# One projection of a fp32 backbone as seven products of quarters, with its weight sums made earlier

## The chip, the cores and the metric

The kernel runs on one core of one Trainium2 chip. The metric is the device time of one execution in microseconds, taken as the median of several. The core has five engines with a queue each: TensorE (PE, with its weight loads as PEld), VectorE (DVE), ScalarE (ACT), GpSimd (POOL) and SyncE (SP), which issues nearly all DMAs here. SBUF is the on-chip memory that all engines read, PSUM holds the matmul results in banks of 128 x 512 floats, DRAM is outside.

## The reference

A trunk of two layers over 1024 latent tokens of width 1024, with a prefix of 256 context tokens. The first layer is windowed attention with a gate:

```python
proj = h_lat @ w_in
q = apply_rope(split_heads(proj[..., :q_end], N_Q_HEADS), cos, sin)
...
o = windowed_attention(q, k, v, kc, vc, sink)      # (1, 1024, 16 heads x 128)
y = (o * jax.nn.silu(z)) @ w_out                   # (1024 x 2048) @ (2048 x 1024)
...
x = x + gate * y
```

The second is a convolution module (a projection to 6144 columns, a depthwise convolution of width 31, a layer norm, a projection back), with the same kind of gate, and a last RMSNorm. Everything is float32. The change concerns `(o * silu(z)) @ w_out`, the output projection of the first layer: 1024 tokens by 2048 inputs by 1024 columns.

## The kernel before

**Numbers.** A float32 matrix is held as a high part (rounded to the format fp32r that TensorE takes in one pass) and a low part (the rest, rounded too). A product is three matmuls: high by high, high by low, low by high. The high part is a cast (`act(..., AF.Copy)` on ACT), the low part a subtraction (`split_lo`, on DVE or POOL). One matmul takes a 128 x 128 block and a 128 x 512 block.

**Memory.** Nearly all tiles are pages, `pg.alloc`: 45 pages of 128 x 1024 words in a queue, given out first freed, first used. A new tile therefore waits for the last reader of the page that it takes over. `hp` holds six smaller ones. PSUM is shared out as two tiles of two banks (`ps_s`, pss in the profile), two of one bank (`ps_g`, psg) and two more (`ps_o`, pso).

**Order.** PE runs in program order (`pin("P")`). The instructions of the other engines and of SP are put in order by a planner, which plays the program through on its own estimate of times; where several are ready on an engine, the one earlier in the program goes first. `tc.high_priority()` lifts an instruction, and `after` ties one behind another.

**Attention** runs 128 steps (8 pairs of heads by 16 blocks of 64 tokens). A step makes the scores of the next block on PE, finds the maximum (DVE), takes the exponential (ACT), scales by the reciprocal sum (POOL, the op to which `anchor_p` points), and transposes the block before (PE, then ACT and DVE). Between them `fill` runs a fixed number of matmuls of the input projection. `low_parts` is a generator that is advanced once in most steps: it loads a page of an output weight, makes its low part (ACT cast and POOL subtraction, two of 512 columns each) and stores it in DRAM, in `wolA` for this projection (16 pages) and `wolC` for the last one (16). The gated attention output is stored in DRAM as `ozd`, 16 blocks of 128 rows by 1024 tokens.

**The output projection**, `proj_attn`, works through `seqB`: four quarters of the output (`h`, the half of the tokens, by `m`, the half of the columns), each of 8 steps `kk` of 256 inputs. A step has 4 token blocks `b` with 6 matmuls each, so 24. `load(i)` brings a page of weights, its low part from `wolA` and, if `m` is 0, a page of rows from `ozd`; `split(i)` makes the high weights (ACT) and, if `m` is 0, the high (ACT) and low rows (DVE). `ahead` runs loads two steps and splits one step ahead in program order. Of the first quarter, blocks 0 and 1 of steps 0 to 6 (`EARLY_ROWS`) are run as fill in the last steps of attention. After step 7 of a quarter, `evac0` takes each block out of PSUM: multiply by the gate (DVE), add the residual (DVE or POOL), store to `x1d`, sum the squares (ACT). After the second quarter of a half it also takes the root, scales the rows (`xn`), and puts eight `turn_in` into `later`: transposes of the normalized rows on PE, for the next layer. `bgA` takes these from `later` between steps and loads the first weights of the convolution (`wsB`). The last three steps (`BYBLOCK`) are run block by block.

**The convolution stage** (`b_mm`) follows: 48 column tiles of 2 x 24 matmuls, with the depthwise convolution on DVE, ACT and POOL beside them, and then the last projection.

In the traces all instructions carry the line of one helper (L91), so they are told apart by their tiles: `wo`, `woh`, `wol` are a weight page and its high and low part, `ozf`, `ozh`, `ozl` the same for the rows, `xr` the residual, `x` the new rows, `xn` the normalized ones, `low` and `lhi` the tiles of `low_parts`.

Of the kernel before, what the change touches and what calls it, by code (L numbers as in the profile page):

```python
# [39 lines left out]
LAST_FILL = (11, 10)  # L40
FIRST_FILL = 48
# [55 lines left out]
def backbone_kernel(  # L97
# [619 lines left out]
    wolA, wolC = (dr.tile([2, NK, P, 2, 512], F32, tag=n, name=n) for n in ("wolA", "wolC"))  # L717
# [7 lines left out]
    def store():  # L725
        while made:
            dst, raw = made.pop()
            SY.dma_start(out=dst, in_=raw)
            pg.free(raw)

    def low_parts():

        items = [(pair_rows(w, m, kk), d[m, kk]) for w, d in ((Wo, wolA), (Wp, wolC)) for m in range(2) for kk in range(NK)]
        his = pg.alloc(F32R, [2, 512], "lhi")
        raws = {}

        def load(i):
            if i < len(items):
                raws[i] = pg.alloc(F32, [2, 512], "low")
                SY.dma_start(out=raws[i], in_=items[i][0])  # L740

        for i, (_, dst) in enumerate(items):
            load(i)
            raw = raws.pop(i)
            store()
            yield "open"
            for b in range(2):
                after(act(his[:, b], raw[:, b], AF.Copy), anchor_a)
                after(split_lo(G, raw[:, b], raw[:, b], his[:, b]), anchor_p)
                if b == 0:  # L750
                    yield "open"
            made.append((dst, raw))
            yield "shut"
        store()
        pg.free(his)

    subs = [(h, m) for h in range(2) for m in range(2)]
# [3 lines left out]
    def proj_attn():  # L761

        st, oz = {}, {}
        todo = {"load": 0, "split": 0}

        def load(i):
            s, kk = seqB[i]
            h, m = subs[s]
            w, wl = pg.alloc(F32, [2, 512], "wo"), pg.alloc(F32R, [2, 512], "wol")
            SY.dma_start(out=w, in_=pair_rows(Wo, m, kk))  # L770
            SY.dma_start(out=wl.bitcast(F32), in_=wolA[m, kk])
            st[i] = [w, wl]
            if m == 0:
                f = pg.alloc(F32, [2, 512], "ozf")
                SY.dma_start(out=f, in_=ozd[2 * kk:2 * kk + 2, :, h * 512:h * 512 + 512].rearrange("a p n -> p a n"))
                oz[(h, kk)] = f

        def split(i):
            s, kk = seqB[i]
            h, m = subs[s]  # L780
# [8 lines left out]
            if m == 0:  # L789
                f = oz[(h, kk)]  # L790
                oh, ol = pg.alloc(F32R, [2, 512], "ozh"), pg.alloc(F32R, [2, 512], "ozl")
                high, low = act(oh, f, AF.Copy), split_lo(V, ol, f, oh)
                if 0 < i < EARLY_ROWS:
                    for ins, ties in ((high, (anchor_z[0:1], anchor_a)), (low, (anchor_z[1:2], anchor))):
                        for t in ties:
                            after(ins, t)
                pg.free(f)
                oz[(h, kk)] = (oh, ol)

        def ahead(i, nl, ns):  # L800
            while todo["load"] <= min(i + nl, len(seqB) - 1):
                load(todo["load"])
                todo["load"] += 1
            while todo["split"] <= min(i + ns, len(seqB) - 1):
                split(todo["split"])
                todo["split"] += 1

        def block(s, kk, b, acc, w, o):
            for e in range(2):
                lh, ll = (t[:, e, b * P:b * P + P] for t in o)  # L810
                for a, c in ((lh, w[0]), (lh, w[1]), (ll, w[0])):
                    PE.matmul(acc, a, c[:, e], start=kk == 0 and e == 0 and a is lh and c is w[0],
                              stop=kk == NK - 1 and e == 1 and a is ll)
                    yield

        for i in range(EA):
            ahead(i, 0, -1)
            yield
        ahead(0, 1, 0)
        yield  # L820
        banks = {4: ps_g(), 5: ps_g()}
        for i in range(EARLY_ROWS):
            ahead(i, min(EA, EARLY_ROWS - 1 - i), min(1, EARLY_ROWS - 1 - i))
            for b in range(2):
                yield from block(0, i, b, banks[4 + b], st[i], oz[(0, i)])
# [5 lines left out]
        xr = None  # L831
        for i, (s, kk) in enumerate(seqB):
            h, m = subs[s]
            acc = [banks[b] for b in ((4, 5, 0, 1), (2, 3, 4, 5), (0, 1, 4, 5), (2, 0, 3, 1))[s]]
            ahead(i, EA, 0)
            if kk == 4:
                xr = [pg.alloc(F32, [2, 512], "xr") for _ in range(2)]
                for b in range(4):
                    SY.dma_start(out=xr[b // 2][:, b % 2],
                                 in_=x[0, (4 * h + b) * P:(4 * h + b + 1) * P, m * 512:m * 512 + 512])  # L840
            w, o = st.pop(i), oz[(h, kk)]
            if i >= len(seqB) - BYBLOCK:
                ahead(i, EA, 1)
                held.append((kk, w, o))
                bgA(s, kk)
                if kk == NK - 1:
                    for b in range(4):
                        for k2, w, o in held:
                            run(block(s, k2, b, acc[b], w, o))
                        evac0(s, b, acc[b], xr)  # L850
                    for k2, w, o in held:
                        pg.free(*w, *o)
                continue
            for b in range(2 if i < EARLY_ROWS else 0, 4):
                run(block(s, kk, b, acc[b], w, o))
                if b == 2:
                    ahead(i, EA, 1)
            pg.free(*w)
            if m:
                pg.free(*oz.pop((h, kk)))  # L860
            bgA(s, kk)
            if kk == NK - 1:
                for b in range(4):
                    evac0(s, b, acc[b], xr)
# [3 lines left out]
    def evac0(s, b, acc, xr):  # L868
        h, m = subs[s]
# [4 lines left out]
        if m == 0:  # L874
# [3 lines left out]
        tt(G if b % 2 and s < len(subs) - 1 else V, t, t, xr[b // 2][:, b % 2], ALU.add)  # L878
# [4 lines left out]
        act(junk[:, 0:512], t, AF.Square, accum_out=ss[:, m:m + 1])  # L883
        hp.free(junk)
        if m == 0:
# [3 lines left out]
        for m in range(2):  # L889
            if b % 2 == 0:  # L890
                x1[("n", m, b // 2)] = pg.alloc(F32, [2, 512], "xn")
            V.tensor_scalar(out=x1[("n", m, b // 2)][:, b % 2], in0=x1[(m, b // 2)][:, b % 2], scalar1=r,
                            scalar2=None, op0=ALU.mult)
# [426 lines left out]
    for i, (pr, st) in enumerate(steps):  # L1320
# [36 lines left out]
        if lstate[0] == "open" or h and (h % 4 < 3 or qb < LOWS):  # L1357
# [543 lines left out]
    def bgA(s, kk):  # L1901
        if s == 2 and kk == 6:
            wsB.load()
            wsB.load()
        if s == 3 and kk >= 5:
            wsB.split()
        for _ in range(2 if kk >= 2 or s == 0 and kk else 0):
# [99 lines left out]
```

## Time and profile before

| | |
|---|---|
| median of 3 executions | 1679.54 us (1678.84 to 1679.65) |
| the profiled execution | 1680.83 us, of which 1679.1 us are its span |
| mean granted TensorE clock | 0.999 |
| DMA, all queues | 244.63 MB in 139607 packets, mean 146 GB/s |

The profile shows one execution, cut into 40 slices of 42 us in its overview. Attention fills the slices up to 800 us, the output projection runs from there to 966 us, the convolution stage to 1494 us, the last projection to the end. A busy time of PE is made up of matmuls that overlap: a single 128 x 512 matmul is shown with 390 ns, while they follow each other faster than that. Idle time before an instruction is put down to the instruction or DMA whose semaphore came last.

### The profile page before, as it was taken

The numbers are of one execution on the slowest core, as the hardware profiler recorded it, in microseconds if no ns is written. First come the engines' busy times: TensorE is split into PE (matmuls) and PEld (weight loads), VectorE is DVE, ScalarE is ACT, GpSimd is POOL, SyncE is SP. The second block draws the span as 40 slices with busy tenths as digits, with TensorE's granted clock in tenths as the row PEclk, the third lists the DMA queues.
The fourth block names the chain that finished last, engine by engine and source line by source line (L and its number), as shares of the span: only waits on it lengthen the run. The fifth ranks groups of instructions, "written<-read, shape, count | busy, mean of one in ns | idle before, by whom it ended". The sixth has DMA issues, their size and how long they took to land.

```text
span 1679.1 us, 23843 instructions
## 1 busy us (share of the span) xinstructions
PE 1666.0 (99%) x8340; PEld 1396.3 (83%) x8340; DVE 1091.2 (65%) x2063; ACT 870.2 (52%) x1523; POOL 874.9 (52%) x831
## 2 busy tenths in 40 slices
PE   9999999999999999999999999999999999999998
PEld 6888888888888888888888788888888888888886
DVE  5755554555455554556234389999999999868832
ACT  5644543555355544546333365555665664566731
POOL 0246673576547564642001268999898887130400
PEclk9999999999999999999999999999999999999999
DMA  9424442444335443457976522020211212387981
GB/s 382 171 62 144 141 144 76 142 154 151 105 125 167 148 129 98 127 159 262 325 247 215 193 88 101 1 76 14 76 50 51 88 38 70 132 276 246 318 288 50
DMA packets 139607, 244.63 MB, mean 146 GB/s; under 512 B 44650, under 2 KB 61346, under 8 KB 139488
## 3 DMA queue, kind: packets, MB, share of 16 engines
q1 hardware_dynamic: 133408, 233.15, 40.7%
q10 hardware_dynamic: 6080, 9.97, 2.4%
q8 instruction: 65, 1.06, 0.2%
q14 instruction: 54, 0.44, 0.1%
HBM read 190.90 MB, written 41.69 MB: 139 GB/s over the span
## 4 chain that ended last, share of the span: by engine, by line
PE 97%; DVE 1%; DMA 1%; POOL 0%; ACT 0%; issue 0%; ACTq 0%; POOLq 0%; DVEq 0%
PE psg L91 50%; PE pss L91 26%; PE pso L91 22%; DMA rope_half<-rope_half 1%; POOL rope_half L91 0%; DVE rq L91 0%; DVE x_page L91 0%; DVE ms L91 0%; DVE rope_half L91 0%; POOL kl_page L91 0%; DVE wlo_page L91 0%; ACT whi_page L91 0%; ACTq L91 0%; ACT rope_half L91 0%; DVE hf_page L91 0%
## 5 line engine op out<-in xcount | busy, mean ns | idle before, releaser
L91 POOL TENSOR_TENSOR odd_half<-odd_half,prod_half 128x513 f32<-128x513 f32 (+2 forms) x252 | 314.5, 1256 | 22.5 <-ACT prod_half L91 9.2
L91 POOL TENSOR_TENSOR wlo_page<-wraw_page,whi_page 128x512 fp32r<-128x512 f32 (+1 forms) x104 | 174.9, 1698 | 157.2 <-ACT whi_page L91 125.7
L91 PE MATMUL psg<-hh_page,whi_page 128*128 128x512 f32 x600 | 236.8, 395 | 0.0
L91 PE MATMUL psg<-hl_page,whi_page 128*128 128x512 f32 x600 | 234.8, 391 | 0.0
L91 PE MATMUL psg<-hh_page,wlo_page 128*128 128x512 f32 x600 | 234.3, 390 | 0.0
L91 ACT ACTIVATE prod_half<-ubuf,dww 128x513 f32<-128x513 f32 (+2 forms) x252 | 165.6, 675 | 116.7 <-POOL odd_half L91 113.0
L91 PE MATMUL psg<-h2h_page,whi_page 128*128 128x512 f32 x464 | 181.9, 392 | 0.0
L91 PE MATMUL psg<-h2h_page,wlo_page 128*128 128x512 f32 x464 | 180.6, 389 | 0.0
L91 PE MATMUL psg<-h2l_page,whi_page 128*128 128x512 f32 x464 | 180.6, 389 | 0.0
L91 DVE SCALAR_TENSOR_TENSOR pss<-ubuf,dww,pss 128x512 f32<-128x512 f32 (+3 forms) x270 | 173.0, 674 | 0.1
L91 DVE SCALAR_TENSOR_TENSOR pss<-ubuf,wsum,pss 128x512 f32<-128x512 f32 (+3 forms) x270 | 172.3, 674 | 0.2
L91 ACT ACTIVATE pt<-pss 128x640 fp32r<-128x640 f32 (+1 forms) x128 | 86.7, 677 | 142.5 <-PE pss L91 142.5
L91 POOL TENSOR_SCALAR p_page<-p_page,sc 128x576 f32<-128x576 f32 (+2 forms) x128 | 93.2, 728 | 106.9 <-DVE sc L91 104.4
L91 ACT ACTIVATE p_page<-p_page,sc 128x577 f32<-128x577 f32 (+2 forms) x128 | 96.9, 757 | 78.6 <-DVE sc L91 76.7
L91 DVE CUSTOM_DVE_ANT_0 p_page<-pss,mask_page,nsink 128x576 f32<-128x576 f32 (+1 forms) x112 | 90.2, 806 | 70.5 <-PE pss L91 57.4
L91 PEld LDWEIGHTS psg<-hh_page,wlo_page 128*128 128x128 f32 x600 | 112.7, 188 | 24.2
L91 PEld LDWEIGHTS psg<-hh_page,whi_page 128*128 128x128 f32 x600 | 112.7, 188 | 19.7 <-ACT hh_page L91 0.3
L91 PEld LDWEIGHTS psg<-hl_page,whi_page 128*128 128x128 f32 x600 | 113.0, 188 | 19.1 <-DVE hl_page L91 0.2
L91 DVE TENSOR_TENSOR pt<-pss,pt 128x640 fp32r<-128x640 f32 (+1 forms) x128 | 100.7, 787 | 36.3 <-ACT pt L91 36.1
L91 ACT ACTIVATE whi_page<-wraw_page 128x1024 fp32r<-128x1024 f32 x88 | 92.6, 1052 | 53.9 <-PE psg L91 19.3
L91 PE MATMUL pso<-h2h_page,whi_page 128*128 128x512 f32 x304 | 118.3, 389 | 0.0
L91 PE MATMUL pso<-h2l_page,whi_page 128*128 128x512 f32 x304 | 118.3, 389 | 0.0
(255 smaller groups left out, 3915.6 us busy)
## 6 DMA issues: line engine op xcount, KB each, us to landing
wraw_page<-in_k_wconv_dram SPq DMA_DIRECT2D x48, 512.0 KB
wraw_page<-in_k_win_dram SPq DMA_DIRECT2D x40, 512.0 KB
wo_page<-in_attn_w_out_dram SPq DMA_DIRECT2D x32, 512.0 KB
wol_page<-wolA SPq DMA_DIRECT2D x32, 512.0 KB
wo_page<-in_conv_w_out_dram SPq DMA_DIRECT2D x32, 512.0 KB
wol_page<-wolC SPq DMA_DIRECT2D x32, 512.0 KB
rope_half<-rope_half ACTq DMA_DIRECT2D x76, 128.0 KB
araw_page<-in_k_ada_dram SPq DMA_DIRECT2D x16, 512.0 KB
```

What stands on the lines that cost most here:

```text
L91: r = f(*a, **k)
```

## The change

The 2 x 2 x 2 partition of the projection has row quarters A11, A12, A21, A22 (half of the tokens by half of the inputs) and weight quarters B11 to B22. Before, each of the four output quarters was the sum of two products of quarters, eight in all. Now seven products are made, in Winograd's form:

- round 0, 8 steps: M1 = A11 B11 (steps 0 to 3), kept; then M2 = A12 B21 (steps 4 to 7). C11 = M1 + M2
- round 1, 4 steps: (A21 + A22 - A11) (B22 - B12 + B11). With M1 it makes U2
- round 2: (A21 + A22) (B12 - B11). With U2 it makes U4
- round 3: (A12 - (A21 + A22 - A11)) B22. C12 = U4 + this
- round 4: (A11 - A21) (B22 - B12). C22 = U4 + this, and U3 = U2 + this
- round 5: A22 (B21 - (B22 - B12 + B11)). C21 = U3 + this

The four weight sums are made in `low_parts`, on POOL, from two pages at a time, and stored in DRAM (`wsums`); the low parts of the second column half of this weight are no longer made there. The row sums are made on DVE in `split`. Rounds 1 to 5 load no low parts: weights and rows are both split in the stage, the weights' low parts on POOL. The kept products are copied or added out of PSUM into pages (`m1`, `u2`, `u4`) and added to the residual, times the gate, on POOL (`joined`). In `evac0` the second half of `xn` moves from DVE to ACT, and POOL adds the residual in the first quarter only. `low_parts` starts three steps earlier in attention.

```diff
+LOAD_TO = {0: (8, 7), 1: (8, 7), 2: (9, 7), 4: (9, 8), 5: (10, 8), 6: (10, 8), 7: (11, 9)}
...
+        u = pair(0)
+        yield "open"
+        for kt in range(KT):
+            store()
+            t = pair(kt + KT)
+            minus(u[:, 1], u[:, 0], u[:, 0])
+            yield "open"
+            minus(t[:, 1], u[:, 1], u[:, 1])
+            yield "open"
+            minus(t[:, 1], u[:, 0], t[:, 1])
+            keep(u, (0, 2), kt)
+            yield "open"
+            store()
+            if kt + 1 < KT:
+                u = pair(kt + 1)
+            minus(t[:, 0], t[:, 1], t[:, 0])
+            keep(t, (3, 1), kt)
+            yield "shut"
...
+    SEQA = [(0, kk) for kk in range(NK)] + [(r, kk) for r in range(1, 6) for kk in range(NK // 2)]
...
+            rows = {1: ((1, kk), (1, k2), (0, kk)), 2: (), 3: ((0, k2),), 4: ((0, kk), (1, kk)), 5: ((1, k2),)}[r]
+            st[i] = [o_raw(*a) for a in rows] + [w_raw(pair_rows(Wo, 1, k2) if r == 3 else
+                                                       wsums[{1: 1, 2: 0, 4: 2, 5: 3}[r], kk])]
...
+            if r == 1:
+                a21, a22, f = rows
+                tt(V, a21, a21, a22, ALU.add)
+                pg.free(a22)
+                tt(V, f, a21, f, ALU.subtract)
+                kept[(1, kk)], kept[(2, kk)] = a21, f
+                keep = True
...
+            act(wh, w, AF.Copy)
+            act(oh, f, AF.Copy)
+            wl, ol = pg.alloc(F32R, [2, 512], "wol"), pg.alloc(F32R, [2, 512], "ozl")
+            for e in range(2):
+                split_lo(G, wl[:, e], w[:, e], wh[:, e])
+            split_lo(V, ol, f, oh)
...
+            start, stop = kk % 4 == 0, kk % 4 == 3
...
+        def joined(us, xrs, m, keep=False):
+            ns = slice(m * 512, m * 512 + 512)
+            for b in range(4):
+                u = us[b // 2][:, b % 2]
+                g = hp.alloc(F32, None, "ug")
+                tt(G, g[:, 0:512], u, gbc0[0][:, ns], ALU.mult)
+                for xr in xrs:
+                    t = xr[b // 2][:, b % 2]
+                    tt(G, t, t, g[:, 0:512], ALU.add)
...
+        order = [(0, 2), (0, 3), (1, 2), (1, 3), (2, 2), (3, 2), (2, 3), (3, 3)]
+        order += [(i, b) for i in range(4, EARLY_ROWS) for b in (2, 3)] + [(7, b) for b in range(4)]
+        acc = [banks[b] for b in (4, 5, 0, 1)]
+        for i, b in order:
+            if b == 2 and i != 3:
+                ahead(*LOAD_TO[i])
...
+            run(block(i, b, acc[b]))
+            if i == 3:
+                act(half_pages(m1, b, "m1"), acc[b], AF.Copy)
+            if b == 3:
+                done(i)
+                bgA(0, i)
+                if i == 4:
+                    joined(m1, [xr], 0, True)
...
+        for i in range(8, len(SEQA)):
+            r, kk = SEQA[i]
+            acc = [banks[b] for b in ((2, 3, 4, 5) if r < 4 else (0, 1, 2, 3))]
+            ahead(i + 3, i)
...
+            if (r, kk) == (3, 1):
+                joined(u4, [xr12, xr22], 1)
...
+            for b in range(4):
+                run(block(i, b, acc[b]))
+                if kk == 3 and r in (1, 2, 4):
+                    with tc.high_priority():
+                        d = {1: u2, 2: u4, 4: u2}[r]
+                        d = half_pages(d, b, "u") if r < 4 else d[b // 2][:, b % 2]
+                        tt(V, d, acc[b], (m1 if r == 1 else u2)[b // 2][:, b % 2], ALU.add)
+                if b == 2:
+                    ahead(i + 3, i + 1)
...
+            if kk == 3 and r > 2:
                 for b in range(4):
+                    evac0(r - 3, 1, b, acc[b], xr12 if r == 3 else xr22)
...
+            if (r, kk) == (4, 3):
+                joined(u2, [xr], 0)
...
-        tt(G if b % 2 and s < len(subs) - 1 else V, t, t, xr[b // 2][:, b % 2], ALU.add)
+        tt(G if b % 2 and h == 0 and first else V, t, t, xr[b // 2][:, b % 2], ALU.add)
...
+            if m:
+                act(d, f, AF.Copy, scale=r)
+            else:
+                V.tensor_scalar(out=d, in0=f, scalar1=r, scalar2=None, op0=ALU.mult)
...
-        if lstate[0] == "open" or h and (h % 4 < 3 or qb < LOWS):
+        if lstate[0] == "open" or i >= 5 and (h % 4 < 3 or qb < LOWS):
```

More of the change, by code (lines that the diff above doesn't have):

```diff
@@ L788, in split @@
             st[i] = (wh, wl)
[L789 to L796, printed above, removed]
+            f = oz[i]
@@ new lines, in residual @@
+        def residual(h, m):
+            xr = [pg.alloc(F32, [2, 512], "xr") for _ in range(2)]
+            for b in range(4):
+                SY.dma_start(out=xr[b // 2][:, b % 2],
+                             in_=x[0, (4 * h + b) * P:(4 * h + b + 1) * P, m * 512:m * 512 + 512])
+            return xr
+        def joined(us, xrs, m, keep=False):
[7 more added lines that the diff above has]
+                    tt(G, t, t, g[:, 0:512], ALU.add)
+                hp.free(g)
+                if b % 2 and not keep:
+                    pg.free(us[b // 2])
@@ L1899, in backbone_kernel, with bgA @@
     projB = proj_out()
-    def bgA(s, kk):
-        if s == 2 and kk == 6:
+    def bgA(r, kk):
+        if (r, kk) == (4, 3):
             wsB.load()
             wsB.load()
-        if s == 3 and kk >= 5:
+        if r == 5 and kk:
             wsB.split()
-        for _ in range(2 if kk >= 2 or s == 0 and kk else 0):
+        for _ in range(2 if r == 0 and kk or r == 4 and kk >= 2 or r == 5 and kk < 2 else 0):
             if later:
```

203 lines of the change are left out of this document (123 added, 80 removed).

## The prediction

> **What bounds the kernel now.** The page comes first: busy shares, slices, and the chain that ended last.
>
> ```profile
> span 1679.1 us, 23843 instructions
> ...
> PE 1666.0 (99%) x8340; PEld 1396.3 (83%) x8340; DVE 1091.2 (65%) x2063; ACT 870.2 (52%) x1523; POOL 874.9 (52%) x831
> ...
> DVE  5755554555455554556234389999999999868832
> ...
> POOL 0246673576547564642001268999898887130400
> PEclk9999999999999999999999999999999999999999
> ...
> PE 97%; DVE 1%; DMA 1%; POOL 0%; ACT 0%; issue 0%; ACTq 0%; POOLq 0%; DVEq 0%
> ```
>
> TensorE is 97% of the chain, at full granted clock throughout. So a matmul taken away is time gained, as long as nothing else becomes late. Slices 19 to 23 are the output projection: DVE and POOL, full in the convolution behind it, stand at 0 to 4 tenths there. Next, the projection's stretches (us, then busy time and instructions of PE, PEld, DVE, ACT, POOL, then clock, DMA share, GB/s).
>
> ```profile
> 804.00:828.50 24.50, 24.50 (x119) 19.88 (x118) 5.50 (x12) 8.15 (x9) 0.65 (x9) 1.00 0.89 321
> 828.50:872.00 43.50, 43.50 (x194) 36.02 (x193) 8.08 (x12) 13.52 (x17) 2.73 (x2) 1.00 0.77 263
> 872.00:920.80 48.80, 48.80 (x233) 40.78 (x232) 25.71 (x54) 21.72 (x34) 8.99 (x7) 1.00 0.64 220
> 920.80:948.00 27.20, 27.20 (x121) 22.52 (x121) 4.36 (x8) 9.29 (x14) 1.71 (x2) 1.00 0.72 264
> 948.00:966.00 18.00, 16.98 (x75) 13.73 (x75) 12.32 (x18) 5.88 (x10) 9.47 (x4) 1.00 0.24 88
> ```
>
> PE waits once, for 1.02 us, in the last stretch. POOL works 23.6 us of 162: room for new work.
>
> **What is removed.** The groups by form (count, busy us, mean ns, idle before) and one piece of the chain of waits (start, us):
>
> ```profile
> L91 PE MATMUL psg<-wol_page,ozh_page 128*128 128x512 f32 x96 | 37.5, 391 | 0.0
> L91 PE MATMUL psg<-woh_page,ozl_page 128*128 128x512 f32 x96 | 37.5, 391 | 0.0
> L91 PE MATMUL psg<-woh_page,ozh_page 128*128 128x512 f32 x96 | 37.4, 390 | 0.0
> L91 PE MATMUL pss<-woh_page,ozh_page 128*128 128x512 f32 x160 | 62.9, 393 | 1.0 <-DVE x_page L91 1.0
> L91 PE MATMUL pss<-wol_page,ozh_page 128*128 128x512 f32 x160 | 62.3, 389 | 0.0
> L91 PE MATMUL pss<-woh_page,ozl_page 128*128 128x512 f32 x160 | 62.3, 389 | 0.0
> ```
>
> ```profile
> 920.79 35.38 PE pss L91 x156
> ```
>
> These are 3 x (96 + 160) = 768 matmuls, 32 steps of 24. The mean of 390 ns is latency, since they overlap; the pace is 35.38 / 156 = 0.2268 us, or 5.44 us a step. The new order has 8 + 5 x 4 = 28 steps, 672 matmuls. Removed: 96 x 0.2268 = **21.77 us**, all on the path. The 84 matmuls inside attention stay as they were; so do the 108 of round 0 behind it (24.5 us). Rounds 1 to 5 then take 20 x 5.44 = 108.8 us, plus 32 transposes of the next input.
>
> **What is added, in the stage.** Every step of rounds 1 to 5 now splits weights and rows into high and low halves itself, where before the low weight half was loaded and rows were split in every second product alone.
>
> ```profile
> L91 POOL TENSOR_TENSOR low_page<-low_page,lhi_page 128x512 f32<-128x512 f32 x64 | 83.1, 1299 | 61.0 <-ACT lhi_page L91 54.0 <-ACT p_page L91 5.4 <-DMA wsum_raw<-in_ada_w_dram 1.6
> L91 ACT ACTIVATE woh_page<-wo_page 128x1024 fp32r<-128x1024 f32 x63 | 66.3, 1055 | 85.0 <-DMA wo_page<-in_conv_w_out_dram 35.9 <-DMA wo_page<-in_attn_w_out_dram 27.2 <-PE psg L91 11.9
> ```
>
> ```profile
> 826.86 0.69 DVE L91 TENSOR_TENSOR x_page<-x_page,xr_page 128x512 f32<-128x512 f32 x1
> ...
> 857.47 1.23 DVE L91 TENSOR_TENSOR ozl_page<-ozf_page,ozh_page 128x1024 fp32r<-128x1024 f32 x1 [12.94 <-PE psg L91]
> ```
>
> - ACT: two casts a step, 2 x 1.06 = 2.1 of 5.44 us; hidden. Half of the xn scalings move here from DVE, also hidden.
> - POOL: two low halves a step, 2 x 1.30 = 2.6 us. The joins add two operations a block for M1 (8, 10.4 us, in round 0), three for U4 (12, 15.6 us, in round 3) and two for U3 (8, 10.4 us, in round 5). Rounds 1 to 5 sum to 20 x 2.6 + 15.6 + 10.4 = 78.0 us, with four h2l (5.2) and two residual adds (2.6) 85.8 of some 112 us. Alone it fits.
> - DVE: one low half a step (1.23) and row sums of the same size: two a step in round 1, one in rounds 3 and 4. That is 32 x 1.23 = 39.4 us, plus 12 sums out of PSUM at 0.69 and evacuations as before. Alone it fits.
>
> The two together are the question, because they do not run side by side:
>
> ```profile
> 952.69 7.68 POOL L91 TENSOR_TENSOR wlo_page<-wraw_page,whi_page 128x1024 fp32r<-128x1024 f32 x3 [28.89 <-DMA wraw_page<-in_k_wconv_dram]
> ```
>
> ```profile
> 952.83 2.82 DVE L91 TENSOR_TENSOR x_page<-x_page,xr_page 128x512 f32<-128x512 f32 x1
> ...
> 956.44 1.49 DVE L91 SCALAR_TENSOR_TENSOR ms<-ssf 128x1 f32<-128x1 f32 x1 [0.79 <-ACT junk_half L91]
> ```
>
> ```profile
> 828.27 1.29 POOL L91 TENSOR_TENSOR x_page<-x_page,xr_page 128x512 f32<-128x512 f32 x1 [23.75 <-DVE x_page L91]
> 831.64 1.67 POOL L91 TENSOR_TENSOR x_page<-x_page,xr_page 128x512 f32<-128x512 f32 x1 [2.08 <-issue]
> ```
>
> A 0.69 us add on DVE takes 2.82 us, ending 0.4 us after the first of the POOL operations (2.56 each) should have ended; a one-column operation takes 1.49, to the end of the second. The other way, 1.29 on POOL becomes 1.67. So DVE operations that read two SBUF tiles and POOL operations wait for each other, whole instructions long. The Trainium skill says the same on its page "SBUF — State Buffer", section "Who interferes with whom": a DVE operation with two SBUF inputs and a GpSimd read exclude each other for the whole instruction. By that rule the sum goes by the joint total below, as these rows do.
>
> The joint total up to where PE can be held up: in the last round the final three steps run block by block, so their splits are due 5.44 + 2.72 = 8.2 us into round 5, that is 87.0 + 3.5 (transposes) + 8.2 = 99 us behind round 0. By then, from full durations: POOL splits and DVE work of 20 steps, 52.0 + 39.4 = 91.4, less two steps of round 1 made in round 0 (2 x 6.3 = 12.6), plus U4's join 15.6, residual adds 2 x 1.3 + 10 x 0.69 = 9.5, h2l 4 x 1.3 + 4 x 0.69 = 8.0: 112 us, 13 too many. But the 2.82 row ended 0.4 us behind its blocker, against 0.69 alone, so about 0.25 us of each operation is start and drain that overlaps. With 18 x 2 + 12 + 2 + 4 = 54 POOL operations on the port, 0.25 less each gives 98 us: full, without overflow. Bounds 0 to 13; I take **4 us** of PE stall, nearer to the lower end, because the 2.82 row speaks for the overlap, and above 0 because a resource that is full to the brim hits some deadlines late.
>
> **Loads.** Round 1 loads four pages a step, 4 x 0.524 MB in 5.44 us, 385 GB/s. The transfers' rate from 804 to 840, in slices of 0.9 us:
>
> ```profile
> GB/s 77 127 259 342 320 331 123 32 173 309 200 262 357 407 389 391 421 410 407 403 410 437 414 423 419 405 401 421 419 398 382 223 259 178 332 412 353 207 255 305
> ```
>
> Pressed, the queue moves about 410 GB/s for 15 us on end. Row 7, round 1 and a residual are 1.6 + 8.4 + 1.0 = 11.0 MB, 27 us, due over some 35. No stall (bounds 0; 7 us at the 263 GB/s of the second stretch). The Trainium skill's page "DMA: Bandwidth & Descriptors", section "Specifications", gives about 358 GB/s as a core's limit to HBM; the row above shows more. By 358 the round's 8.4 MB would take an estimated 23.4 us against 21.8, 1.6 us late without the early loads.
>
> **What is added in attention.** POOL low operations become 32 differences and 24 x 2 low halves, 80 in place of 64: 16 x 1.30 = 20.8 us over 640 us of a POOL that is half busy; ACT loses 16 casts. SP carries 8.4 MB more, and its stores queue behind POOL as before. What PE lost there so far:
>
> ```profile
> PE pss L91 <- POOL p_page L91: 1.6, 1, 1.6
> ```
>
> One wait in 128 steps: the softmax has slack. A POOL operation queued behind the scaling delays the next scaling by 1.3 us at most. I take 0.5 us (bounds 0 and 20.8). M1's copy out of PSUM is a new wait for PE, since step 4 restarts the bank: ACT sits in the softmax queue, and behind ACT's copy wait its exp and transposed copies. Inside attention six matmuls (1.4 us) lie between, against a copy of about 0.6 us:
>
> ```profile
> L91 ACT ACTIVATE pt<-pss 128x512 fp32r<-128x512 f32 x32 | 19.0, 595 | 24.9 <-PE pss L91 24.9
> ```
>
> I take 0.5 us for all four (bounds 0 and 4 x 1.06, one cast ahead of each). Behind the stage U3's join feeds the last evacuations; PE meets them again in the transposes two steps (10.9 us) into the convolution, so that much lateness costs nothing. Banks between rounds have three blocks (4.1 us) against 0.69 on DVE: nothing. The convolution starts earlier with everything it feeds on, so it only shifts; a gain or loss of 2 us by reordering is the bound.
>
> **Sum.** 21.77 - 4 - 0.5 - 0.5 = 16.77 us. The profiled execution took 1680.83 (span 1679.1), 1.3 above the median of 1679.54. 1680.83 - 16.77 = 1664.1; on the median's scale 1679.54 - 16.77 = **1662.8**.
>
> **Rivals.**
> - *Clean*: the splits run so far ahead that nothing is late. Against it: kept sums leave fewer free pages. For it: before, rows of the second half (due at 872, the third stretch above) were cast 30 us ahead:
>
> ```profile
> 842.22 1.06 ACT L91 ACTIVATE ozh_page<-ozf_page 128x1024 fp32r<-128x1024 f32 x1 [0.29 <-DMA ozf_page<-ozd]
> ```
>
>   1679.54 - 21.77 = 1657.8.
> - *POOL's queue order*: U4's 12 joins (15.6 us) run ahead of the split of round 3's third step, due 10.9 us into the round and then done at 15.6 + 2.6 = 18.2: 7.3 us. U3's 8 joins ahead of the last three splits: 10.4 + 7.8 - 8.2 = 10.0. Together 17.3: 1675. For it: both joins stand ahead of these splits in the program; against it: the planner starts what is ready first.
> - *The other side, the shared port without overlap*: from round 1 on, every DVE sum waits out a POOL operation. Full durations for the rounds are 112 + 10.4 (U3) + 2.5 (two convolution splits) = 125 against 112, and each of the 32 DVE operations that meets a POOL one in flight waits on average 0.65 us: 21 more, in DVE's queue ahead of evacuations. 13 + 21 = 34 at worst, 1692; it decides once more than 21.8 us of it, two thirds, reach PE. With three quarters, 26 us, it gives 1684. Against it: DVE is idle enough to wait.
> - *Attention pays*: the added 20.8 us of POOL lie on the path: 1678, no gain. Against it: the single wait above.
>
> **Chances.** Forecast (1660 to 1668) 0.50; clean 0.22; POOL's order 0.14; port 0.08; attention 0.03; in between 0.03. A measurement of this kernel can tell about 0.2%, 3.4 us. Faster by more: 0.87, within: 0.05, slower: 0.08. The range runs from clean less 1.3 to POOL's order nearly whole: 1656.5 to 1674, leaving out the port, attention and the end of POOL's order.
>
> **What would show it.** 672 matmuls on woh and wol tiles of this product; PE's idle time in rounds 1 to 5 by releaser: wol (POOL) or ozl (DVE) for the port; wol alone in rounds 3 and 5 for the queue's order; ozf or wo DMA for loads; xn for late evacuations. POOL and DVE means there above 1.30 and 1.23 show the exclusion. If PE idles under 1 us in the stage, clean was right; if attention's end shifts past 804, POOL there was mispriced.

## The result, and the profile after

The changed kernel takes 1705.05 us (median of 4, 1702.51 to 1705.29), the kernel before 1679.60 beside it (4 runs, 1678.84 to 1679.72): a ratio of 1.0149, interval 1.0131 to 1.0167. It is 25.5 us slower, where 1662.8 was predicted with a range of 1656.5 to 1674. The profiled execution took 1705.04 us, span 1703.3.

The page of the changed kernel: totals, slices of PE, DVE and POOL, granted clock by slice.

```profile
span 1703.3 us, 23865 instructions
...
PE 1657.2 (97%) x8244; PEld 1385.0 (81%) x8244; DVE 1155.3 (68%) x2099; ACT 876.3 (51%) x1527; POOL 1002.7 (59%) x911
...
PE   9999999999999999999799699999999999999998
...
DVE  5755554555355544565657979999999999867832
...
POOL 0247673666547573742659857999898888130300
PEclk9999999999999999999799899999999999999999
```

The 96 matmuls are gone (8340 to 8244). What is new stands in slices 19 and 22 of PE: 7 and 6 tenths, with the clock down to 7 and 8 tenths there. Where it was lost is read off one instruction, the first matmul of the convolution stage (start, duration), before and then after:

```profile
965.46 0.39 PE L91 MATMUL psg<-h2h_page,whi_page 128*128 128x512 f32 x1
```

```profile
989.67 0.39 PE L92 MATMUL psg<-h2h_page,whi_page 128*128 128x512 f32 x1
```

It comes 24.21 us later, and the span is 24.2 longer: all of the loss lies ahead of it. As 21.8 us of matmuls were taken out there, 46 us of something else came in. A little of it is attention's: the first matmul behind attention starts at 805.55 us, before at 803.87, so 1.7 later. The rest belongs to the projection's stage, from that matmul to the first of the convolution: 184.1 us, before 161.6. PE's waits over the whole span (us in all, times, longest):

```profile
PE pss L92 <- ACT m_page L92: 11.0, 2, 9.8
PE pso L92 <- DVE ssf L92: 6.8, 1, 6.8
PE pss L92 <- DVE u_page L92: 6.1, 4, 2.3
PE pss L92 <- DVE x_page L92: 5.5, 3, 2.4
PE pso L92 <- DVE xn_page L92: 3.3, 2, 2.7
...
PE pss L92 <- POOL p_page L92: 2.0, 2, 1.8
```

Before, the stage had one wait of 1.0. The first five rows sum to 32.7 us. Most of the rest of the 46 goes with the clock: in the stage PE is busy for 20.8 us at half clock, where a matmul takes 0.43 us in place of 0.2268, an estimated 10 us lost. The longest wait shows how it comes about. First the timeline of PE at it, then the stretches around it (us, busy of PE, PEld, DVE, ACT, POOL, clock, DMA share, GB/s):

```profile
824.51 0.79 PE L92 MATMUL pss<-woh_page,ozh_page 128*128 128x512 f32 x1 [9.81 <-ACT m_page L92]
825.10 0.63 PE L92 MATMUL pss<-wo_page,ozh_page 128*128 128x512 f32 x1
825.53 0.63 PE L92 MATMUL pss<-woh_page,ozl_page 128*128 128x512 f32 x1
```

```profile
814.00:824.00 10.00, 0.70 (x4) 0.24 (x2) 7.00 (x7) 3.09 (x4) 2.57 (x2) 0.65 0.73 241
824.00:836.00 12.00, 10.29 (x28) 7.39 (x29) 5.50 (x8) 2.95 (x4) 9.01 (x7) 0.50 0.89 284
836.00:840.00 4.00, 4.00 (x16) 3.17 (x15) 2.91 (x2) 0.96 (x1) 4.00 (x2) 0.82 1.05 393
840.00:864.00 24.00, 24.00 (x108) 19.88 (x107) 19.58 (x18) 12.89 (x19) 20.48 (x11) 1.00 0.74 245
```

PE stood 9.81 us, and went on at 0.43 us a matmul (825.53 less 825.10) in place of 0.2268. Why it stood is told by ACT's timeline, and ACT's by DVE's:

```profile
814.07 1.06 ACT L92 ACTIVATE ozh_page<-ozf_page 128x1024 fp32r<-128x1024 f32 x1 [9.00 <-DMA ozf_page<-ozd]
815.03 1.04 ACT L92 ACTIVATE woh_page<-wo_page 128x1024 fp32r<-128x1024 f32 x1
822.92 1.06 ACT L92 ACTIVATE ozh_page<-ozf_page 128x1024 fp32r<-128x1024 f32 x1 [6.84 <-DVE ozf_page L92]
823.88 0.58 ACT L92 ACTIVATE m_page<-pss 128x512 f32<-128x512 f32 x1
```

```profile
817.89 1.91 DVE L92 TENSOR_TENSOR ozf_page<-ozf_page,ozf_page 128x1024 f32<-128x1024 f32 x1 [1.51 <-DMA ozf_page<-ozd]
820.13 1.23 DVE L92 TENSOR_TENSOR ozf_page<-ozf_page,ozf_page 128x1024 f32<-128x1024 f32 x1 [0.33 <-DMA ozf_page<-ozd]
821.28 0.47 DVE L92 COPY dww<-pso 128x124 f32<-128x124 f32 x2
821.67 2.35 DVE L92 TENSOR_TENSOR ozf_page<-ozf_page,ozf_page 128x1024 f32<-128x1024 f32 x2
```

M1's copy takes 0.58 us, but stands in ACT's queue behind the cast of a row of round 1, which waits for DVE's row sums, which wait for the DMA of the rows. The waiting matmul isn't the restart of the copied bank, as one might think. That bank belongs to block 2; the matmul is still one of M1, step 2 of block 3, in the other bank of the same two-bank tile, and the program gives it a wait on ACT's copy.

### The profile page after: what moved, and what is told of

Read it like the earlier page. It is cut to its first block, busy times and chain, and to the rows that moved or that the text cites. A ratio compares the mean times of both kernels' runs of the same rounds, so it can differ in the third digit from the quotient of the medians.

```text
span 1703.3 us, 23865 instructions
## 1 busy us (share of the span) xinstructions
PE 1657.2 (97%) x8244; PEld 1385.0 (81%) x8244; DVE 1155.3 (68%) x2099; ACT 876.3 (51%) x1527; POOL 1002.7 (59%) x911
## 5 line engine op out<-in xcount | busy, mean ns | idle before, releaser
L92 PE MATMUL pso<-h2h_page,wlo_page 128*128 128x512 f32 x304 | 118.4, 390 | 0.0
```

The source lines that it names most:

```text
L92: r = f(*a, **k)
```

## The experiments

Each ran once, beside the kernel before on the same chip (1678.84 to 1679.53); "after" is the changed kernel, 1705.05. Four runs of it span 2.8 us, so smaller differences are not read.

**The wait on M1's copy.** Theory: PE waits for the bank that is restarted.

*e1_own_banks*, M2's blocks 2 and 3 in banks of their own:

```diff
                 act(half_pages(m1, b, "m1"), acc[b], AF.Copy)
+                acc[b] = banks[b]
...
-            acc = [banks[b] for b in ((2, 3, 4, 5) if r < 4 else (0, 1, 2, 3))]
+            acc = [banks[b] for b in ((0, 1, 4, 5) if r < 4 else (2, 3, 0, 1))]
```

> The changed kernel, with M2 of blocks 2 and 3 accumulated in two free PSUM banks, so that TensorE does not wait there for M1's copy. Theory (the copy stands in ScalarE's queue behind a cast that waits for a row sum): the 11.0 us of waits on m_page go, and with them the half clock behind them (about 14 us of half speed, 8 us), so 1705 - 19 = 1686. Rival (the loads are late whatever waits for them): TensorE waits in round 1 for its first row sums instead, 1698 to 1705.

1708.06 us, and the wait on m_page stays at 10.0. The theory falls. It led to the reading above: the matmul that waits is in the tile being read.

*e5_m1_tile* copies a tile only after both of its banks are done, with e1's banks:

```diff
-            if i == 3:
-                act(half_pages(m1, b, "m1"), acc[b], AF.Copy)
+            if (i, b) == (3, 3):
+                for c in (2, 3):
+                    act(half_pages(m1, c, "m1"), acc[c], AF.Copy)
+                    acc[c] = banks[c]
```

> The changed kernel, with both copies of M1's blocks 2 and 3 issued behind step 3 of both blocks, and M2 of these blocks in the other two-bank PSUM tile. Theory (a matmul into one bank of a two-bank tile waits for a reader of the other bank, so step 2 of block 3 waited for the copy of block 2): the 11.0 us of waits on m_page go, with the half clock behind them: 1684 to 1690. Rival (late loads): the idle time comes back in round 1 as waits on ACT woh or ozh, POOL wol or DVE ozl, 1698 to 1706.

1706.37 us. PE's waits in it:

```profile
PE pss L92 <- DVE u_page L92: 11.7, 4, 7.7
...
PE pso L92 <- DVE dww L92: 4.1, 1, 4.1
```

m_page is gone from the list, which shows the tile as the reason for that wait. But its 11 us came back: 4.1 on the copy of the convolution's taps (dww), which stands behind the same row sums on DVE, and 5.6 more on the additions for U. The rival was right: a victim was removed, not the lateness.

**The clock.** *e2_spin* and *e7_spin_ahead* put 44 matmuls whose results are not used into the wait, in e2 ahead of block 2 of step 4, in e7 ahead of the matmul that waits. The edit of e7:

```diff
+            if (i, b) == (2, 3):
+                for _ in range(44):
+                    PE.matmul(banks[2], st[6][0][:, 0, 0:P], oz[6][0][:, 0], start=True, stop=True)
             run(block(i, b, acc[b]))
```

> The changed kernel, with 44 added matmuls (10.0 us at full clock) into an unused bank just ahead of the matmul that waits for M1's copy; their result is not used. Theory (the half clock comes from TensorE standing idle): the wait stays but is filled, the granted clock stays at 1.00 from 814 to 840 us, and about 8 us are gained, 1697. Rival (the clock falls for another reason, or the slow stretch costs nothing because loads set the pace there): 1705, or up to 1715 where the added matmuls lie on the path.

> The changed kernel, with 44 added matmuls (10.0 us at full clock) into an unused bank ahead of step 2 of block 3, which is the matmul that waits for M1's copy; their result is not used. Theory (the half clock comes from TensorE standing idle): the wait is filled, the granted clock stays at 1.00 through 840 us, and 6 to 9 us are gained on the changed kernel's 1705: 1696 to 1699. Rival (loads set the pace in that stretch): 1703 to 1706.

e2 took 1711.12 us: its matmuls stood behind the wait, which stayed at 9.2, so it tells nothing of the clock. e7 took 1709.42. Its stretches:

```profile
814.00:824.00 10.00, 10.00 (x45) 8.29 (x45) 7.83 (x8) 2.96 (x4) 2.79 (x3) 1.00 0.82 270
824.00:836.00 12.00, 10.60 (x51) 8.24 (x50) 8.72 (x8) 2.49 (x3) 12.00 (x8) 1.00 0.98 359
...
840.00:864.00 24.00, 21.02 (x92) 16.76 (x90) 18.07 (x17) 13.55 (x19) 20.65 (x12) 1.00 0.64 213
```

The clock stays at 1.00 through the wait, and nothing is gained: PE, at full pace from 824 on, waits again by 864, where the changed kernel, after its half pace, is busy throughout (24.00 of 24.00 us from 840 to 864). The stage takes 183.9 us, as good as the changed kernel's 184.1; the 4.4 us by which e7 is slower lie in the convolution and behind it (718.7 us from its first matmul to the end, 713.6 in the changed kernel). So the slow clock in round 0 is a consequence of waiting, and cost nothing of its own here, where the data for round 1 were later still.

**Tiles and joins.** *e6_tiles*: e5, and each addition for U issued after both banks of its tile are done (`for c in {1: (0, 1), 2: (2,), 3: (3,)}.get(b, ())`), and round 5's banks in the order 4, 2, 5, 3, so that its evacuations alternate between tiles. *e8_tiles_evac*: also the joins moved from POOL into the evacuation on DVE, where the kept product is added straight to PSUM:

```diff
-    def evac0(h, m, b, acc, xr):
+    def evac0(h, m, b, acc, xr, us):
...
-        tt(V, t, acc, gbc0[0][:, ns], ALU.mult)
+        tt(V, t, acc, us[b // 2][:, b % 2], ALU.add)
+        tt(V, t, t, gbc0[0][:, ns], ALU.mult)
...
-                    joined(m1, [xr], 0, True)
...
-                joined(u4, [xr12, xr22], 1)
...
-                joined(u2, [xr], 0)
```

*e12_taps_later*: e8 with the taps' transposes in round 2, one a step.

> As e5_m1_tile, and besides the sums out of PSUM in rounds 1, 2 and 4 are issued behind the second block of a two-bank tile, and round 5 alternates between tiles. Theory (shared tiles cause the waits on u_page, 6.1 us, and x_page, 5.5 us, too): these go as well, 1668 to 1676. Rival (they come from DVE being late whichever tile is next): the waits stay within 3 us of 11.6, 1682 to 1690.

> As e6_tiles, and M1, U4 and U3 are added in the evacuation on DVE, straight from PSUM, in place of the joins on POOL (28 POOL operations less, 16 DVE operations more). Theory (POOL and DVE hold each other up in rounds 3 to 5, which delays the scaled rows that the transposes wait for): the waits on ssf and xn, 10.1 us, shrink below 4: 1660 to 1668. Rival (DVE is the bound by its own count of operations): as e6_tiles or slower.

> As e8_tiles_evac, with the taps' transposes (whose bank is freed by a copy on DVE that stands behind a row sum) moved from round 0 to round 2. Theory (in-order queues pass the wait for round 1's rows on to whatever short instruction stands behind): the wait on dww, 4.6 us, goes and 2 to 5 us are gained, 1689 to 1692. Rival (it comes back as another wait): 1693 to 1695.

1696.02, 1694.18 and 1695.57. The tiles are worth 9.0 us, about a quarter of what was expected; with the joins it is 10.9, too little more to be read. The 10.9 is what is left of a larger gain: e8's stage is 14.9 us shorter (169.2), and from the convolution on it takes 4.7 longer (718.3). In e12 the wait on dww goes, and u_page rises from 9.0 to 12.1 us, with one of 9.2: passed on again.

**The preparation of rounds 1 to 5.** Four runs that start from the changed kernel. *e3_no_joins* leaves out the joins of U4 and U3 (both `joined` calls become `pg.free`); *e4_no_row_sums* the four `tt(V, ...)` of the row sums; *e11_dve_splits* leaves out nothing, but makes the weights' low halves on DVE:

```diff
-            for e in range(2):
-                split_lo(G, wl[:, e], w[:, e], wh[:, e])
             split_lo(V, ol, f, oh)
+            split_lo(V, wl, w, wh)
```

*e16_after_loads_only* leaves out the row sums and, with `G.memset(wl.bitcast(F32), 0.0)` in place of POOL's two subtractions, the weights' low halves.

> The changed kernel without the joins of U4 and U3 into the residuals (20 POOL operations of rounds 3 to 5): three of the four output quarters lack these terms. Theory (POOL and DVE hold each other up in rounds 3 to 5): most of TensorE's 22 us of waits behind 850 us go, and the half clock around 965 us with them: 1688 to 1692. Rival (DVE's own work is too much): 1702 to 1705.

> The changed kernel without the 16 row sums on DVE: rows are split as they are loaded, so that products 3 to 6 are of other matrices. Theory (DVE's sums stand in the way twice: ahead of the cast before M1's copy, and against POOL later): about half of both waits goes, 1685 to 1692. Rival (late loads and POOL alone set the waits): 1700 to 1705.

> The changed kernel with only one thing altered: the weights' low halves in rounds 1 to 5 are made on DVE, one subtraction of 128x1024 in place of two of 128x512 on POOL. Theory (shared port): faster than 1705 although DVE gets 20 operations more, 1688 to 1697. Rival (DVE is the bound by its own count): 1705 to 1715.

> The changed kernel itself (its tiles and joins as they are) with the four row sums and the weights' low halves left out, as in e13. Port as the main cause: 1705.05 - 13.3 - 13.5 = 1678, 1674 to 1682, the rest of the 46 us being the tiles and late loads. If tiles and loads are the main cause: 1688 to 1692, no better than the run without row sums (1691.75).

1695.39 (9.7 off), 1691.75 (13.3), 1698.49 (6.6) and 1689.03 (16.0). e4 came within what its theory gave; e3 and e11 fell just short of theirs. e11 is the most telling: it puts 20 more instructions on DVE, which is 68% busy in the changed kernel's stage (126.0 of 184.1 us), and is faster. But row sums and splits together give 16.0, hardly more than the sums alone, as the side of tiles and loads had it. Its waits tell why:

```profile
PE pss L92 <- ACT m_page L92: 6.9, 2, 4.2
PE pss L92 <- DVE u_page L92: 4.4, 4, 1.6
```

The tile waits remain, so the same two cuts were made in e8's order: *e9_no_pool_split* (the memset alone), *e13_loads_only* (memset, and no row sums). *e10_all_dve* does the whole computation, with none of the stage's work on POOL: e8 with e11's split, the other POOL instructions of the stage on DVE, and e12's taps.

> As e8_tiles_evac (1694), with the 40 subtractions on POOL that make the weights' low halves in rounds 1 to 5 replaced by 20 memsets to zero, which read nothing from SBUF; the low halves of these weights are left out of the products. Theory (the shared reads of POOL and DVE set the pace of rounds 1 to 5): DVE operations go back to 1.23 us from 2.3 and the waits on u_page, hf and xn mostly go, 1668 to 1676. Rival (late pages and loads set the pace): 1690 to 1695.

> As e8_tiles_evac, with everything that POOL did in the stage moved to DVE (weights' low halves as one 128x1024 subtraction, residual adds, h2l), and the taps' transposes moved from round 0 to round 2. Theory (a pair of pages costs the shared port 1.23 us on DVE and 2.6 on POOL, so DVE alone is faster than both): 1662 to 1674. Rival (DVE's count of operations is the bound: round 1 has some 31 us for it against 21.8 of TensorE): 1685 to 1700.

> The tiles and the joins of the run e8 (1694.18), with the four row sums left out and the weights' low halves left out (a memset in place of POOL's two subtractions), so that of the preparation in rounds 1 to 5 only the loads, ACT's casts and DVE's low half of the rows remain. If the sums and the splits set the pace of the stage, both go: e4 gave 13.3 and e9 gave 13.5, so 1694.2 - 26.8 = 1667, 1662 to 1672. If loads that land late set it, nothing is gained over e9 (1680.66): 1677 to 1682, with PE waits that end in ACT's casts or DVE's splits behind ozf or wo loads.

1680.66, 1691.63 and 1675.02; e9 and e13 lie between what the theory and the rival gave. POOL's subtractions cost 13.5 us here (1694.18 - 1680.66), the row sums 5.6 more. What stands behind the 13.5 is in the groups by form from 804 to 965 (count, busy us, mean ns of one), in the changed kernel and then in e9:

```profile
L92 DVE TENSOR_TENSOR ozl_page<-ozf_page,ozh_page 128x1024 fp32r<-128x1024 f32 x21 | 33.8, 1610 | 26.5 <-ACT ozh_page L92 18.7 <-POOL wol_page L92 3.7 <-issue 1.6
L92 DVE TENSOR_TENSOR ozf_page<-ozf_page,ozf_page 128x1024 f32<-128x1024 f32 x16 | 26.4, 1658 | 18.9 <-DMA ozf_page<-ozd 15.9 <-PE psg L92 2.9
...
L92 POOL TENSOR_TENSOR wol_page<-wo_page,woh_page 128x512 fp32r<-128x512 f32 x40 | 68.0, 1724 | 35.5 <-ACT woh_page L92 17.8 <-issue 8.1 <-DMA xr_page<-in_x_dram 4.1
```

```profile
L92 DVE TENSOR_TENSOR ozl_page<-ozf_page,ozh_page 128x1024 fp32r<-128x1024 f32 x21 | 25.6, 1221 | 15.6 <-ACT ozh_page L92 8.7 <-PE psg L92 5.7 <-POOL h2l_page L92 1.1
L92 DVE TENSOR_TENSOR ozf_page<-ozf_page,ozf_page 128x1024 f32<-128x1024 f32 x16 | 20.6, 1292 | 24.2 <-DMA ozf_page<-ozd 12.8 <-PE psg L92 9.6 <-issue 1.7
```

Beside POOL's reads DVE's splits and sums take 1610 and 1658 ns, without them 1221 and 1292 (in e8, which differs from e9 in the splits alone, 1544 and 1523); POOL's take 1724, where the same shape took 1299 in the kernel before. That is 21 x 0.39 + 16 x 0.37 + 40 x 0.42 = 31 us more of busy time in the changed kernel. It isn't work: an instruction that waits for the other engine's is shown as busy, as the last section shows on single ones. But the queue behind it stands meanwhile. Giving DVE everything doesn't help enough: e10's instructions take 1.22 us, and its stage is 6.3 us shorter than e8's (162.9), but 3.5 of that are lost again from the convolution on (721.8), and its stretches are short of DVE:

```profile
830.00:850.00 20.00, 17.78 (x78) 14.07 (x77) 18.93 (x25) 12.61 (x18) 0.00 (x0) 1.00 0.71 253
...
930.00:950.00 20.00, 11.66 (x51) 9.29 (x52) 19.54 (x30) 9.69 (x17) 0.00 (x0) 0.81 0.27 92
```

DVE is 95% and 98% busy there, PE 89% and 58%.

**The loads.** *e14_one_load_less* is e8, *e15_load_no_pool* e9, each with the third row page of round 1 left out and the second used in its place; the sums keep their number.

```diff
-            rows = {1: ((1, kk), (1, k2), (0, kk)),
+            rows = {1: ((1, kk), (1, k2)),
```

> As e8 (1694.18), but round 1 loads three pages a step and not four: the third row page is left out and the page of the second is used in its place, so the sums and splits stay in number and size, with other values. If the sums and splits set the pace: within 2 us of e8, 1692 to 1696. If round 1 is late because its pages land late: 5 us or more off in round 1, 1685 to 1690.

> As e9 (1680.66: e8 without the weights' low halves), with round 1's third page left out as in e14. With POOL off the port, what is left in round 1 is loads and DVE's sums. If loads: 1673 to 1677. If DVE's sums alone: 1679 to 1682.

1696.11 and 1688.92: with a quarter of round 1's loads less, no gain in e14 and 8.3 us lost in e15. Neither theory had the loss. DVE's timeline in e15 shows one thing that came between, and PE's the wait from it, in e15 and then, at the same place, in e9:

```profile
815.37 1.23 DVE L92 TENSOR_TENSOR ozl_page<-ozf_page,ozh_page 128x1024 fp32r<-128x1024 f32 x1 [12.36 <-ACT ozh_page L92]
816.51 0.68 DVE L92 SCALAR_TENSOR_TENSOR oz_half<-pso,zs_page 128x512 f32<-128x512 f32 x1
```

```profile
817.25 1.06 PE L92 MATMUL pso<-ident,dwr_page 32*128 32x32 f32 x8 [5.59 <-DVE oz_half L92]
```

```profile
819.72 1.06 PE L92 MATMUL pso<-ident,dwr_page 32*128 32x32 f32 x8 [4.80 <-DVE dww L92]
```

The planner had swapped two instructions. The last output of attention (oz_half) stands behind a low half whose row was late, and PE waits 5.59 us for oz_half (5.4 in e14). In e9, without the swap, the same matmuls wait 4.80 us for dww, behind late rows too: once more the wait has another name, and the swap itself costs 0.8 us. Of the other 7.5 us, 1.7 lie in attention, which ends later, and 3.9 in waits on u_page (7.7 in place of 3.8); what made them longer stays open. So these two runs do not answer for the loads. Of the loads e13 says more: with sums and POOL splits out, the same loads arrive in time for PE to be full from 850 to 894, the first two rows of the next view.

**The turn from round 4 to round 5.** e13 has PE full in the rounds where the work was taken out, and empty at the end (same columns as above):

```profile
850.00:872.00 22.00, 22.00 (x99) 18.22 (x98) 7.72 (x9) 7.28 (x9) 3.08 (x4) 1.00 0.94 356
872.00:894.00 22.00, 22.00 (x99) 18.23 (x98) 6.38 (x8) 7.23 (x7) 3.83 (x5) 1.00 0.29 95
...
916.00:938.00 22.00, 14.85 (x67) 11.85 (x65) 19.41 (x31) 12.43 (x20) 7.93 (x5) 0.90 0.33 119
```

With neither sums nor POOL splits DVE is still 88% busy from 916 to 938. Before, the output quarters left PSUM eight steps apart; now three of them leave at the ends of rounds 3, 4 and 5, four steps apart, each with an addition more in e8's order, and the transposes of the next input fall into the same stretch. *e17_loads_spread* is e13 and *e18_tiles_spread* e8, with the transposes thinned out:

```diff
-        for _ in range(2 if r == 0 and kk or r == 4 and kk >= 2 or r == 5 and kk < 2 else 0):
+        for _ in range(2 if r == 0 and kk or r == 5 and kk >= 2 else 1 if r == 4 and kk >= 2 or r == 5 else 0):
```

> As e13 (1675.02; row sums and the weights' low halves left out), with the transposes of the next input spread: one a step from round 4's third step on and two in round 5's last two, where it was two a step in four steps. What e13 still waits for is 3.0 us on u_page and 4.3 on hf_page at the turn of rounds 4 and 5, followed by a stretch at a granted clock of 0.50, where two sets of evacuations and the transposes' copies meet on DVE. If that crowding is the cause: both waits go and 4 to 10 us with them, 1665 to 1671. If the transposes come too late for the convolution instead, or the wait moves on: 1674 to 1680.

> As e8 (1694.18), with the transposes spread as in e17. The same crowding, with sums and splits there: hf_page's 5.2 us go, 1686 to 1691. If DVE is late there with or without them: within 2 us of e8, 1692 to 1696, with another name in the wait.

1669.03 and 1689.38: 6.0 and 4.8 us off, as the crowding expected. In e17 what is left is still there:

```profile
804.00:828.50 24.50, 24.48 (x118) 19.81 (x117) 6.39 (x11) 6.78 (x8) 4.18 (x12) 1.00 0.71 249
...
916.00:938.00 22.00, 16.72 (x77) 13.02 (x76) 21.49 (x34) 10.06 (x19) 8.68 (x5) 0.92 0.16 57
```

Round 0 has no wait, and from 916 to 938 DVE is 98% busy and PE 76%.

One path from the time without stalls to the changed kernel, each step a pair of runs:

| step | us | what it adds |
|---|---|---|
| prediction's *clean* | 1657.8 | |
| e17 | 1669.03 | 11.2: in part evacuations on DVE at the turn of rounds 4 and 5 |
| e13 | 1675.02 | 6.0: transposes in the same place |
| e9 | 1680.66 | 5.6: row sums on DVE |
| e8 | 1694.18 | 13.5: weights' low halves on POOL |
| after | 1705.05 | 10.9: two-bank tiles and joins on POOL |

The shares depend on the way taken: out of the changed kernel itself the row sums give 13.3 and sums and splits together 16.0, on this path 19.1. Of the 11.2 the stretch from 916 to 938 accounts for 5.3 us, in which PE is idle; 1.4 lie in attention, which ends at 805.3, and 1.0 from the convolution on. What moving the evacuations would give was not tried, and the number of pages, which the kept sums draw on, was not varied. No run that does the whole computation beats the kernel before; the nearest, e18, is 10.5 us slower than the run of it beside (1678.84).

## Why the prediction was wrong

- **What is removed**, 21.77 us on the path: right. 96 matmuls are gone, and where nothing is late the others keep their pace: in e13 PE runs 99 matmuls in 22.00 us, twice in a row. No run got the whole of it.
- **"I take 4 us of PE stall"**, bounds 0 to 13, for the shared port: this is the step that failed. Measured, sums and POOL splits are worth 16.0 to 19.1 us. That DVE and POOL exclude each other was right, and so was the overlap: where they alternate, a pair comes every 2.24 us in place of 1.22 + 1.30, so 0.28 us of each pair is hidden, near the 0.25 that one row gave. Two other things were wrong. DVE's instructions were counted as 32, but 20 low halves and 8 + 4 + 4 row sums make 36 (the rows above have 21, one of them round 0's, and 16): 4.9 us were missing, so that the working's own totals were not 98 and 112 us against 99 but 103 and 117: bounds of some 4 to 18, not 0 to 13. And the total was held against one deadline, 99 us behind round 0, as if work could be done at any time before it. The work has a deadline at every step: the sums are needed in rounds 1, 3 and 4, the evacuations in the last three, and neither could be made earlier, for want of loaded rows or of finished products. e17 and e18 show it for one part: the same transposes, only spread, gave 6.0 and 4.8 us. A total that just fits says little where its parts are bunched.
- **M1's copy, "0.5 us for all four"**, bounds to 4.2: 11.0 in two waits. The bound counted one cast ahead of the copy, by duration, and not what that cast waits for. The six matmuls counted as cover lie in attention; the two copies behind it, where the order goes on in the other bank of the tile, were not looked at.
- **"Banks between rounds have three blocks ... nothing"**: 6.1 us on u_page and 5.5 on x_page. Cover was counted per bank, while the program waits per tile of two banks, and 0.69 us on DVE was taken as if DVE were free.
- **"Loads: no stall"**: half right. Where sums and POOL splits are out, the loads come in time (e13), so their rate alone isn't the limit; but late rows held DVE and ACT in their order with short work behind them: DVE waited 15.9 us for ozf loads in the stage.
- **The clock** was taken as 1.00 throughout. It fell to 0.50 after long waits; in round 0 that alone cost nothing (e7).
- **Attention**, 0.5 us: it ended 1.7 us later, at 805.55 and so past 804, the sign that the prediction had named for POOL being mispriced there (0.5 to 3.7 later in the experiments). PE's waits on p_page rose from 1.6 to 2.0, and a wait of 0.8 on acc_a is new.
- **The convolution only shifts**: right for the changed kernel, 24.21 against 24.2; not for e8 and e10, which lose 4.7 and 8.2 us there.
- **Rivals.** The other side, the shared port, had the direction and the place, at 8%. Its price for the port, 26 to 34 us, was above the 16.0 to 19.1 measured, and it denied an overlap that is there; it gave 1684, 1692 at worst, and came no nearer to 1705 because it had neither the tiles nor the turn of rounds 4 and 5. That it came nearest of all is in part luck. POOL's queue order saw the joins (e3: 9.7) but not that DVE would share the bill. The range left out the side that came.

## What to carry to other kernels

An engine that is idle in the average can't take work that is due in bursts: set new work against the stretch between its inputs' arrival and its due time, round by round, and count two engines that exclude each other as one. In a queue that runs in order, the price of a short new instruction is what the one ahead of it waits for, so follow that chain to its DMA. And where a wait comes from general lateness, taking its victim away passes it on (e5, e12): look for the late data first.

## What the runs showed of the hardware

- A two-input DVE operation and a POOL operation beside it wait for each other and are shown as busy meanwhile: 1610 in place of 1221 ns and 1724 in place of 1299 ns in the mean of the stage, single ones 2.31 us in place of 1.22. DVE's and then POOL's timeline:

```profile
847.91 2.31 DVE L92 TENSOR_TENSOR ozl_page<-ozf_page,ozh_page 128x1024 fp32r<-128x1024 f32 x1
...
850.21 2.25 DVE L92 TENSOR_TENSOR ozf_page<-ozf_page,ozf_page 128x1024 f32<-128x1024 f32 x1
```

```profile
849.10 2.27 POOL L92 TENSOR_TENSOR x_page<-x_page,xr_page 128x512 f32<-128x512 f32 x1
```

  The three end at 850.22, 851.37 and 852.46: POOL 1.15 us behind DVE, DVE 1.09 behind POOL. So the pair takes 2.24 us, and the 2.31 + 2.27 shown for it are 1.22 + 1.30 of work, less an overlap of 0.28, and waiting.

- The clock fell soon and returned late. In the changed kernel, in stretches of 2 us around the longest wait:

```profile
814.00:816.00 2.00, 0.70 (x4) 0.24 (x2) 0.84 (x1) 1.93 (x2) 0.00 (x0) 1.00 0.20 47
816.00:818.00 2.00, 0.00 (x0) 0.00 (x0) 0.49 (x2) 0.07 (x1) 1.84 (x2) 0.74 0.74 250
...
836.00:838.00 2.00, 2.00 (x7) 1.56 (x6) 1.97 (x2) 0.00 (x0) 2.00 (x2) 0.64 1.03 397
838.00:840.00 2.00, 2.00 (x11) 1.61 (x10) 0.94 (x1) 0.96 (x1) 2.00 (x1) 1.00 1.08 389
```

PE went idle at 814.7 and was at half clock from about 817.0, 2.3 us later; it resumed at 824.51 and was back at full clock at about 837.4, 12.9 us later. It had not been busy all that time: after 6.8 us of matmuls, eight 32 x 32 transposes among them, it stood again for 1.2 us, until 832.49, and the clock came back 5.0 us after that. The Trainium skill's page "TensorE: Matmul & The Clock Gate", section "What's actually happening", has both turns after a window of about 3.4 us, idle for the fall and busy for the return. The fall came sooner here, 2.3 us after the last matmul. The return came later, and whether the pause and the small transposes account for that no run here shows.
